# RWKV-7 time mixing on one core: a written-out order ahead of the keys, and the gate's low-rank input mixed on VectorE

## The chip, the cores and the metric

The kernel runs on one core of a Trainium2 chip. A core has a matrix engine (TensorE, PE; its weight loads are listed as PEld), a vector engine (VectorE, DVE), an activation engine (ScalarE, ACT), a general engine (GpSimd, POOL) and a queue engine (SyncE, SP) that issues the loads here. Each engine works through its own queue in order and waits on semaphores for the others. The metric is the time of one execution in microseconds (us), the median of several runs.

## The reference

A two-layer decoder trunk on 256 tokens of width 1024 in float32. Layer 0 is FFN, RWKV-7 time mixing, FFN; layer 1 is FFN, sliding-window attention, FFN. The change lies between layer 0's first FFN and the keys of its time mixing. What is computed there:

```python
h = h + 0.5 * rms_norm(swiglu(rms_norm(h, g[0]), ...), g[1])     # end of the first FFN
u = rms_norm(h, g[2])

x_prev = jnp.pad(x, ((0, 0), (1, 0), (0, 0)))[:, :-1]            # x is u
xx = x_prev - x
xr, xw, xk, xv, xa, xg = [x + xx * mu[i] for i in range(6)]
r = xr @ w_rkv[0]
k = xk @ w_rkv[1]
v = xv @ w_rkv[2]
w = -jax.nn.softplus(-(w0 + jnp.tanh(xw @ w1) @ w2)) - 0.5
decay = jnp.exp(-jnp.exp(w.astype(f32)))
a = jax.nn.sigmoid(a0 + (xa @ a1) @ a2)
g = jax.nn.sigmoid(xg @ g1) @ g2
```

w1 and a1 have 64 columns each, g1 has 128. Behind it come a scan over the tokens and the output product, which the change does not touch.

## The kernel before

The 256 tokens are worked on as two halves of 128 (index `i`), the width of 1024 as eight groups of 128 (index `k`). A product of full precision is made from three reduced ones (`mm3`: the operand is split into a high part, by a cast on ACT, and a low part, by a subtraction on DVE); the low-rank products and the values use plain float32 operands.

The stage of the change, in the order of the code:

- `ffn_tail(i)` ends the first FFN of half `i` in two PSUM banks. `post(i, ...)` squares them on ACT for the norm (L258), multiplies them by the gain on DVE (L259), takes the root through POOL (`rstd`, L239 and L242), adds to the residual `h` (L264) and squares that for the next norm (L266).
- `tm_in(i, stat)` normalises `h` (`normed`, L299), transposes it on PE (L309), writes `u` from the transposed bank with its gain, alternately on ACT (L543, even groups) and DVE (L546, odd groups), and then the difference to the token before, `xx` (L550, L552).
- `mix` makes u + xx * mu on DVE, one instruction for a group of 128 (L520): `xv` for the values, `xkm` (tag `xth`) for the keys.
- `tm_lora(i)` makes the three low-rank inputs as one matrix of 256 columns, w1, a1 and g1 side by side (`lora1`). It does not mix first: because (u + xx * mu) @ W = u @ W + xx @ (mu * W), it multiplies u by W and xx by a copy of W scaled by mu, which `tm_consts` prepared on DVE during the FFN (L511). That is 2 column groups x 8 x 2 = 32 products for a half. ACT then takes tanh into `hwa`, copies the a part into it and takes the sigmoid of the gate part into `sgT` (L583 to L585).
- `v_half(0, xv)` is the first quarter of the values: 8 products of 512 columns (L617). Its weights lie in four buffers (`wr`), which the keys' weights (`w_k`) take over one by one as these products end.
- In `tm_core`, ACT casts the keys' input to `xtl` and DVE subtracts it into `xkl` (L640, L641). PE makes the decay's pre-activation (L659, ACT's sigmoid L660), the a-gate's (L665, L667) and sums of decays (L674, exponentials L677 and L678). Then come the keys' products (L227 with `wk`), whose weights are split on ACT and DVE as they arrive (`k_split`, L314 and L315).

A scheduler with its own time estimates places the instructions of this stage on each engine. From the keys on, a written list (`STEPS`) sets the order, and `in_order` pins it: it ties each instruction of the named engines to the one before it in the program. Loads go out on SP's queue in order: a gain row for the norm after the time mixing (the buffer of the gain that L259 reads last), then the keys' weights. In the stage the first three half-chunk splits of the keys (`wk`) stand on ACT and DVE ahead of the second half's `u`.

Of the kernel before, what the change touches and what calls it, by code (L numbers as in the profile page):

```python
# [8 lines left out]
F32 = mybir.dt.float32  # L9
F32R = mybir.dt.float32r  # L10
AF = mybir.ActivationFunctionType
ALU = mybir.AluOpType
# [4 lines left out]
P = 128  # L17
D = 1024
T = 256
KT = 8  # L20
# [57 lines left out]
class Trunk:  # L78
# [426 lines left out]

    def tm_consts(self):
        nc = self.nc
        u, x = self.l1 = [self.tl("l1", [P, KT, 256], tag=f"l1{j}") for j in range(2)]
        self.load(u, self.a["lora1"].rearrange("p (k c) -> p k c", k=KT), self.mid)
        for j, c0, cw in ((1, 0, 64), (4, 64, 64), (5, 128, 128)):  # L510
            nc.vector.tensor_tensor(x[:, :, c0:c0 + cw], u[:, :, c0:c0 + cw],  # L511
                                    self.cols[:, C_MU + j * 8:C_MU + j * 8 + 8].unsqueeze(2).to_broadcast([P, KT, cw]),
                                    op=ALU.mult)
        nc.gpsimd.memset(self.hwa[64:65, 0, :], 1.0)
        nc.gpsimd.memset(self.hwa[0:64, 1, :], 0.0)
        nc.gpsimd.memset(self.hwa[0:1, 1, :], 1.0)
# [14 lines left out]

    def tm_in(self, i, stat):
        nc = self.nc
        xn, hs = stat
        r = self.rstd([hs[:, 0:1], hs[:, 1:2]], RMS_EPS)
        self.normed(i, r, None, xn)
        sl = slice(i * P, (i + 1) * P)
        for q in range(2):
# [32 lines left out]
            self.nc.tensor.matmul(b[:, j * T:(j + 1) * T], ws[k // 4][:, c0:c0 + P], xf[:, k, :], start=(k == 0),  # L571
                                  stop=(k == KT - 1))

    def tm_lora(self, i):
        nc = self.nc
        sl = slice(i * P, (i + 1) * P)
        bs = [self.bank()[:, 0:P] for _ in range(2)]
        for e, (l, x) in enumerate(zip(self.l1, (self.uT, self.xx))):
            for j in range(2):
                for k in range(KT):  # L580
                    nc.tensor.matmul(bs[j], l[:, k, j * P:(j + 1) * P], x[:, k, sl], start=(k == 0 and not e),  # L581
                                     stop=(k == KT - 1 and e == 1))
        nc.scalar.activation(self.hwa[0:64, 0, sl], bs[0][0:64, :], AF.Tanh)  # L583
        nc.scalar.copy(self.hwa[64:128, 1, sl], bs[0][64:128, :])
        nc.scalar.activation(self.sgT[:, sl], bs[1], AF.Sigmoid)  # L585

    def tm_core(self):
        nc, a, DC = self.nc, self.a, self.DC
        mm = nc.tensor.matmul
        TT, STT = nc.vector.tensor_tensor, nc.vector.scalar_tensor_tensor  # L590
# [12 lines left out]
        xv = self.tl("xt", [P, KT, P], tag="xv0")  # L603
        xkm = self.tl("xt", [P, KT, T], tag="xth")
        xkh = self.tl("xt", [P, KT, T], F32R, tag="xtl")
        self.mix(xv, 3, toks[0])
        self.mix(xkm[:, :, toks[0]], 2, toks[0])
        self.tm_lora(0)
        def v_half(n, x):
            acc = self.bank()  # L610
            ns = slice(n * 512, n * 512 + 512)

            def part(k2):
                w = self.pp.tile([P, 2, 512], F32, name=f"wr{self.uid()}", tag="wr", bufs=4)
                self.load(w, a["w_v"][2 * k2:2 * k2 + 2, :, ns].rearrange("k p c -> p k c"))
                for k in range(2):
                    mm(acc, x[:, 2 * k2 + k, :], w[:, k, :], start=(k2 + k == 0), stop=(k2 + k == 4))  # L617
            return acc, [lambda k2=k2: part(k2) for k2 in range(4)]

        def run(todo):  # L620
            for x in todo:
                x()

        acc0, todo = v_half(0, xv)
        run(todo)
        self.mix(xkm[:, :, toks[1]], 2, toks[1])
        self.tm_lora(1)
        self.close("g2k", "t4", "W1", "W2", "l1", "sh0")
        self.open("sh1")
        self.tl("sh1", [P, 24])  # L630
# [839 lines left out]
    def run(self, out):  # L1470
# [25 lines left out]
        self.load(self.cst[:, P:], a["consts"][:, P:], self.mid)  # L1496
        self.tm_consts()
        g_post = self.gain(R_NORM[(0, 1)], self.mid)
        for i in range(2):
            self.tm_in(i, self.post(i, self.ffn_tail(i), g_post, True))  # L1500
        accs, g_post = self.tm_core()

        g_pre = self.gain(R_NORM[(0, 4)])
        xt = self.new_xt("xt")
# [117 lines left out]
```

## Time and profile before

| | us |
|---|---|
| Median of 3 runs | 1054.13 |
| The three runs | 1054.13, 1053.63, 1066.59 |
| The profiled execution: its time | 1054.67 |
| The profiled execution: its span | 1052.9 |
| Mean granted TensorE clock in it | 0.993 |

The span runs from the first to the last instruction; the other 1.77 us lie around it. In a timeline row stand the start, the length, engine, line of the kernel, operation, output and input tiles, the count, and in brackets the idle time before it with the engine and line that ended it. A row of several instructions covers them all, and instructions of one engine overlap a little, so durations from start to start are the ones to add.

### The profile page before, as it was taken

To read this page: it belongs to the slowest core of one execution; us is meant where nothing else is said; L and a number is where in the kernel's file an instruction comes from. 1 tells how busy PE (TensorE), PEld (TensorE's weight loads), DVE (VectorE), ACT (ScalarE), POOL (GpSimd) and SP (SyncE) were. 2 spreads that over 40 slices of the span, in tenths; PEclk is the share of its full clock that TensorE was granted. 3 is DMA by queue.
4 is the path that set the end of the run, shared out by engine and by line. 5 is a ranking of instruction groups with operands and counts; after the bars stand their busy time and mean duration, and the time that the engine had idled before them with its cause. 6 is when DMAs were issued, how large, how long until landed. Compare 5 with 4: busy or idle time off the path is not lost.

```text
span 1052.9 us, 16152 instructions
## 1 busy us (share of the span) xinstructions
PE 1024.4 (97%) x6264; PEld 860.9 (82%) x6264; DVE 699.4 (66%) x1125; ACT 564.9 (54%) x1014; POOL 20.5 (2%) x34
## 2 busy tenths in 40 slices
PE   6999999999999999999999999999999989999997
PEld 5888888779967887888888788888877668888886
DVE  6666655527798877766665676666668866765652
ACT  6655554365245546655455665555556755655541
POOL 0000000000000001000000000000010000000000
PEclk9999999999999999999999999999999989999999
DMA  8768664034354336766663386676535127766621
GB/s 285 242 195 279 221 193 168 24 117 142 120 171 132 124 134 206 260 199 205 196 184 124 114 268 215 205 241 190 179 111 169 41 82 258 244 216 191 189 81 40
DMA packets 52668, 183.04 MB, mean 174 GB/s; under 512 B 5744, under 2 KB 6000, under 8 KB 52464
## 3 DMA queue, kind: packets, MB, share of 16 engines
q1 hardware_dynamic: 52304, 181.49, 53.3%
q8 instruction: 49, 0.80, 0.3%
q10 hardware_dynamic: 288, 0.52, 0.1%
q14 instruction: 27, 0.22, 0.1%
HBM read 180.94 MB, written 1.05 MB: 173 GB/s over the span
## 4 chain that ended last, share of the span: by engine, by line
PE 90%; ACT 3%; DVE 3%; DMA 2%; issue 1%; POOL 0%; SPq 0%; DVEq 0%; POOLq 0%; ACTq 0%
PE bk L227 35%; PE bk L362 13%; PE bt L362 13%; PE bt L363 7%; PE bk L363 7%; PE bk L571 3%; PE bk L617 2%; PE bk L581 1%; ACT W L195 1%; DMA wr<-in_w_in_dram 1%; PE bc L1002 1%; PE bk L1053 1%; PE bt L309 1%; DVE W L201 1%; DMA wr<-in_w_in_lead_dram 1%
## 5 line engine op out<-in xcount | busy, mean ns | idle before, releaser
L201 DVE TENSOR_TENSOR W<-wr,W 128x1024 fp32r<-128x1024 f32 x280 | 341.1, 1224 | 190.1 <-ACT W L195 188.7
L195 ACT CAST W<-wr 128x1024 fp32r<-128x1024 f32 x280 | 291.9, 1049 | 189.9 <-issue 94.3
L227 PE MATMUL bk<-W,g2k 128*128 128x512 f32 x1056 | 246.0, 390 | 0.0
L227 PEld LDWEIGHTS bk<-W,g2k 128*128 128x128 f32 x1056 | 195.8, 188 | 40.1
L362 PE MATMUL bk<-xtl,W 128*128 128x512 f32 x296 | 105.1, 393 | 0.0
L362 PE MATMUL bt<-xtl,W 128*128 128x512 f32 x296 | 104.4, 391 | 0.3 <-DVE xtl L350 0.3
L362 PE MATMUL bt<-xth,W 128*128 128x512 f32 x296 | 104.5, 390 | 0.0
L362 PE MATMUL bk<-xth,W 128*128 128x512 f32 x296 | 104.3, 390 | 0.0
L363 PE MATMUL bt<-xth,W 128*128 128x256 f32 x296 | 83.5, 282 | 0.0
L363 PE MATMUL bk<-xth,W 128*128 128x256 f32 x296 | 83.5, 282 | 0.0
L363 PE MATMUL bk<-xtl,W 128*128 128x256 f32 x296 | 83.4, 282 | 0.0
L363 PE MATMUL bt<-xtl,W 128*128 128x256 f32 x296 | 83.4, 282 | 0.0
L227 PE MATMUL bk<-W,xtl 128*128 128x512 f32 x216 | 61.7, 434 | 6.4 <-ACT W L195 3.3
L362 PEld LDWEIGHTS bt<-xtl,W 128*128 128x128 f32 x296 | 55.6, 188 | 12.3 <-DVE xtl L350 0.7
L362 PEld LDWEIGHTS bk<-xtl,W 128*128 128x128 f32 x296 | 55.6, 188 | 12.2
L362 PEld LDWEIGHTS bk<-xth,W 128*128 128x128 f32 x296 | 55.6, 188 | 11.6
L362 PEld LDWEIGHTS bt<-xth,W 128*128 128x128 f32 x296 | 55.5, 188 | 11.6
L227 PEld LDWEIGHTS bk<-W,xtl 128*128 128x128 f32 x216 | 42.9, 204 | 20.3 <-ACT W L195 3.8
L363 PEld LDWEIGHTS bk<-xtl,W 128*128 128x128 f32 x296 | 55.8, 189 | 1.2
L363 PEld LDWEIGHTS bt<-xth,W 128*128 128x128 f32 x296 | 55.9, 189 | 0.1
L363 PEld LDWEIGHTS bt<-xtl,W 128*128 128x128 f32 x296 | 55.9, 189 | 0.1
L363 PEld LDWEIGHTS bk<-xth,W 128*128 128x128 f32 x296 | 55.9, 189 | 0.0
(287 smaller groups left out, 1374.7 us busy)
## 6 DMA issues: line engine op xcount, KB each, us to landing
wr<-in_w_in_dram SPq DMA_DIRECT2D x148, 512.0 KB, 3.9
wr<-in_w_out_dram SPq DMA_DIRECT2D x88, 512.0 KB, 3.6
wr<-in_w_in_lead_dram SPq DMA_DIRECT2D x28, 512.0 KB, 4.1
wr<-in_w_v_dram SPq DMA_DIRECT2D x16, 512.0 KB, 3.9
gain<-in_rows_dram SPq DMA_DIRECT2D x13, 512.0 KB, 4.5
wr<-in_w_k_dram SPq DMA_DIRECT2D x8, 512.0 KB, 4.1
wr<-in_w_r_dram SPq DMA_DIRECT2D x8, 512.0 KB, 3.6
wr<-in_w_o_dram SPq DMA_DIRECT2D x8, 512.0 KB, 4.3
```

The costliest lines, as they stand in the source:

```text
L195: self.follow(nc.scalar.copy(w[:, 0, :], raw), 0)
L201: self.follow(nc.vector.tensor_tensor(w[:, 1, :], raw, w[:, 0, :], op=ALU.subtract), 1)
L227: mm = lambda *x, **y: self.nc.tensor.matmul(*x, **y, **kw)
L309: t = self.nc.tensor.transpose(b[:, k * P:(k + 1) * P], xn[:, c:c + P], self.ident)
L362: mm(banks[j], hi[:, c0:c0 + P], xt[c][:, :, k4, :], start=(k == 0), stop=False)
L363: use[0] = mm(banks[j][:, 0:T], lo[:, c0:c0 + P], xt[c][:, 0, k4, :], start=False, stop=(k == KT - 1))
L571: self.nc.tensor.matmul(b[:, j * T:(j + 1) * T], ws[k // 4][:, c0:c0 + P], xf[:, k, :], start=(k == 0), stop=(k == KT - 1))
L581: nc.tensor.matmul(bs[j], l[:, k, j * P:(j + 1) * P], x[:, k, sl], start=(k == 0 and not e), stop=(k == KT - 1 and e == 1))
L617: mm(acc, x[:, 2 * k2 + k, :], w[:, k, :], start=(k2 + k == 0), stop=(k2 + k == 4))
L1002: mm(b[r, m * N:(m + 1) * N], W[r, v - hh * 16, :], XV[r, v, :], start=True, stop=True)
L1053: mm(out[hh][half[1 - e], m * N:(m + 1) * N], lhs, UV[part][:, hh * 16 + q, :], start=(not i and part == 0 and m == 0), stop=(part == e), ...
```

## The change

The stage gets a function of its own, `front`, and its order is pinned on PE, DVE and ACT with `in_order`, from the first half's `tm_in` on. In it:

- The gate's low-rank input is mixed on DVE into a tile `xg` (8 instructions for a half), and `gate` multiplies it by g1 (8 products). `low` makes the decay and a-gate parts as before, 16 products for a half. `tm_consts` no longer scales g1, and the scaled copy is half as large.
- The second half's post-norm is written out inside `front`, cut by the mixes of the first half: four value mixes, the gain product, four value mixes, the residual, four gate mixes, the statistics, four gate mixes. `tm_in` takes the finished root.
- The value products come directly after the first half's `low`, then the first half's gate, then the second half.
- Both sigmoids of the gate come at the end, and the keys' sixteen mixes after everything else.

The diff:

```diff
 def tm_consts(self):
-        u, x = self.l1 = [self.tl("l1", [P, KT, 256], tag=f"l1{j}") for j in range(2)]
+        u, x = self.l1 = [self.tl("l1", [P, KT, 256 - 128 * j], tag=f"l1{j}") for j in range(2)]
...
-        for j, c0, cw in ((1, 0, 64), (4, 64, 64), (5, 128, 128)):
+        for j, c0, cw in ((1, 0, 64), (4, 64, 64)):
...
 def tm_in(self, i, stat):
-        xn, hs = stat
-        r = self.rstd([hs[:, 0:1], hs[:, 1:2]], RMS_EPS)
+        xn, r = stat
...
-    def tm_lora(self, i):
...
+    def front(self, acc1, g_post, xv, xkm, v00):
+        nc = self.nc
+        mm, TT, STT = nc.tensor.matmul, nc.vector.tensor_tensor, nc.vector.scalar_tensor_tensor
+        toks = [slice(0, P), slice(P, T)]
+        xg = self.tl("l1", [P, KT, P], tag="xg")
+
+        def mixes(dst, j, i, ks):
+            for k in ks:
+                self.mix_into(nc.vector, dst[:, k], j, k, toks[i])
+
+        def low(i):
+            b = self.bank()[:, 0:P]
+            for e, (l, x) in enumerate(zip(self.l1, (self.uT, self.xx))):
+                for k in range(KT):
+                    mm(b, l[:, k, 0:P], x[:, k, toks[i]], start=(k == 0 and not e), stop=(k == KT - 1 and e == 1))
+            return b
+
+        def gate():
+            b = self.bank()[:, 0:P]
+            for k in range(KT):
+                mm(b, self.l1[0][:, k, P:2 * P], xg[:, k, :], start=(k == 0), stop=(k == KT - 1))
+            return b
+
+        def low_out(i, b):
+            nc.scalar.activation(self.hwa[0:64, 0, toks[i]], b[0:64, :], AF.Tanh)
+            nc.scalar.copy(self.hwa[64:128, 1, toks[i]], b[64:128, :])
+
+        lo0 = low(0)
...
+        mixes(xv, 3, 0, range(4))
+        for n, sl in enumerate(cols):
+            nc.scalar.activation(xn[:, sl], acc1[n], AF.Square, scale=1.0 / 16, accum_out=ss[:, n:n + 1])
+            TT(og[:, sl], acc1[n], g_post[:, sl], op=ALU.mult)
+        r = self.rstd([ss[:, 0:1], ss[:, 1:2]], 4 * RMS_EPS)
+        mixes(xv, 3, 0, range(4, 8))
+        v00()
+        low_out(0, lo0)
+        for n, sl in enumerate(cols):
+            STT(h[:, sl], og[:, sl], r, h[:, sl], op0=ALU.mult, op1=ALU.add)
+            nc.scalar.activation(xn[:, sl], h[:, sl], AF.Square, scale=1.0 / 32, accum_out=hs[:, n:n + 1])
+        mixes(xg, 5, 0, range(4))
+        r = self.rstd([hs[:, 0:1], hs[:, 1:2]], RMS_EPS)
+        mixes(xg, 5, 0, range(4, 8))
+        g0 = gate()
+        self.tm_in(1, (xn, r))
+        lo1 = low(1)
+        mixes(xg, 5, 1, range(8))
+        low_out(1, lo1)
+        g1 = gate()
+        for i, b in enumerate((g0, g1)):
+            nc.scalar.activation(self.sgT[:, toks[i]], b, AF.Sigmoid)
+        for i in range(2):
+            mixes(xkm[:, :, toks[i]], 2, i, range(8))
...
 def tm_core(self, acc1, g_post, begin):
-        self.mix(xv, 3, toks[0])
-        self.mix(xkm[:, :, toks[0]], 2, toks[0])
-        self.tm_lora(0)
...
-        acc0, todo = v_half(0, xv)
-        run(todo)
-        self.mix(xkm[:, :, toks[1]], 2, toks[1])
-        self.tm_lora(1)
+        v0 = []
+
+        def v00():
+            acc, todo = v_half(0, xv)
+            v0.append(acc)
+            run(todo)
+
+        self.front(acc1, g_post, xv, xkm, v00)
+        acc0 = v0[0]
+        self.in_order(begin, "PE", "DVE", "Activation")
...
 def run(self, out):
-        for i in range(2):
-            self.tm_in(i, self.post(i, self.ffn_tail(i), g_post, True))
-        accs, g_post = self.tm_core()
+        xn, hs = self.post(0, self.ffn_tail(0), g_post, True)
+        r = self.rstd([hs[:, 0:1], hs[:, 1:2]], RMS_EPS)
+        acc1 = self.ffn_tail(1)
+        begin = len(nc.cur_bb.bb.instructions)
+        self.tm_in(0, (xn, r))
+        accs, g_post = self.tm_core(acc1, g_post, begin)
```

How it moves the engines' instructions, at three places. The rows have the line, the operation, output tile and inputs, the size and the count.

PE before, from the end of the first half's low-rank products to the start of the second's (`u`, `xx` the inputs, `l` the low-rank matrices, `bk` and `bt` PSUM banks, `xv` the values' input, `wr` their weights, `t` the normalised rows):

```order
L581 MATMUL bk_1805<-xx_100,l_252_1616 128x128 x4
L581 MATMUL bk_1806<-xx_100,l_252_1616 128x128 x6
L617 MATMUL bk_1842<-wr_1843,xv_272_1786 128x512 x2
L617 MATMUL bk_1842<-wr_1847,xv_272_1786 128x512 x2
L617 MATMUL bk_1842<-wr_1851,xv_272_1786 128x512 x2
L617 MATMUL bk_1842<-wr_1855,xv_272_1786 128x512 x2
L309 MATMUL bt_1760<-cst,t_264_1742 128x128 x4
L309 MATMUL bt_1770<-cst,t_264_1742 128x128 x4
```

PE now, from the first half's low-rank products to the first decay product (`xg` the gate's mixed input, `hwa` the low-rank output):

```order
L587 MATMUL bk_1749<-u_99,l_251_1615 128x128 x8
L587 MATMUL bk_1749<-xx_100,l_252_1616 128x128 x8
L657 MATMUL bk_1785<-wr_1786,xv_264_1745 128x512 x2
...
L593 MATMUL bk_1819<-xg_1748,l_251_1615 128x128 x8
L309 MATMUL bt_1830<-cst,t_272_1769 128x128 x4
L309 MATMUL bt_1840<-cst,t_272_1769 128x128 x4
L587 MATMUL bk_1850<-u_99,l_251_1615 128x128 x8
L587 MATMUL bk_1850<-xx_100,l_252_1616 128x128 x8
L593 MATMUL bk_1877<-xg_1748,l_251_1615 128x128 x8
L705 MATMUL bk_1955<-gain_1739,hwa 128x512
```

The low-rank products of a half went to two banks, one for decay and a-gate, one for the gate; now only the first is left beside u and xx, and the gate's eight products on `xg` follow later, the first half's between the values and the second half's transposes.

DVE before, from the first mixes to the second half's `u` (`xth` and `xkl` the keys' input and its low part, `wk` the keys' weights):

```order
L520 SCALAR_TENSOR_TENSOR xv_272_1786<-xx_100,cols,u_99 128x128 x4
L520 SCALAR_TENSOR_TENSOR xth_1787<-xx_100,cols,u_99 128x128 x3
L299 TENSOR_SCALAR t_264_1742<-h_65,rs_1755 128x512 x2
L520 SCALAR_TENSOR_TENSOR xth_1787<-xx_100,cols,u_99 128x128
L641 TENSOR_TENSOR xkl_1940<-xth_1787,xtl_1788 128x8x128
L315 TENSOR_TENSOR wk_2022<-wr_2020,wk_2022 128x512
L315 TENSOR_TENSOR wk_2038<-wr_2020,wk_2038 128x512
L315 TENSOR_TENSOR wk_2055<-wr_2053,wk_2055 128x512
L546 TENSOR_SCALAR u_99<-bt_1760,cols 128x128
```

DVE now, over the same stretch:

```order
L608 TENSOR_TENSOR t_271_1768<-bk_456,gain_1623 128x512
L239 SCALAR_TENSOR_TENSOR rs_1778<-ss_1766 128x1
L520 SCALAR_TENSOR_TENSOR xv_264_1745<-xx_100,cols,u_99 128x128 x4
L614 SCALAR_TENSOR_TENSOR h_65<-t_271_1768,rs_1778,h_65 128x512 x2
L520 SCALAR_TENSOR_TENSOR xg_1748<-xx_100,cols,u_99 128x128 x4
L239 SCALAR_TENSOR_TENSOR rs_1812<-hs_1767 128x1
L520 SCALAR_TENSOR_TENSOR xg_1748<-xx_100,cols,u_99 128x128 x4
L299 TENSOR_SCALAR t_272_1769<-h_65,rs_1812 128x512 x2
L315 TENSOR_TENSOR wk_2022<-wr_2020,wk_2022 128x512
L315 TENSOR_TENSOR wk_2038<-wr_2020,wk_2038 128x512
L315 TENSOR_TENSOR wk_2055<-wr_2053,wk_2055 128x512
L545 TENSOR_SCALAR u_99<-bt_1830,cols 128x128 x2
```

The keys' mixes and their subtraction left this stretch, the second half's post-norm and the gate's mixes came in, and the three splits of the keys' weights still stand ahead of the second half's `u`.

ACT now, from the second half's low-rank output to the decay's sigmoids (`p` their output, `xtl` the cast of the keys' input):

```order
L597 ACTIVATE hwa<-bk_1850 64x128
L598 COPY hwa<-bk_1850 64x128
L626 ACT_TABLE_LOAD
L626 ACTIVATE sgT<-bk_1819 128x128
L626 ACTIVATE sgT<-bk_1877 128x128
L686 CAST xtl_1747<-xth_1746 128x8x128
L706 ACTIVATE p_303_1954<-bk_1955 128x512
L706 ACTIVATE p_303_1954<-bk_1958 128x512
L686 CAST xtl_1747<-xth_1746 128x8x128
L706 ACTIVATE p_306_1961<-bk_1962 128x512
```

Before, the table load stood between the first half's `hwa` and `sgT`, and both casts came before the decay's sigmoids; now all three stand here, a cast ahead of each pair of sigmoids.

More of the change, by code (lines that the diff above doesn't have):

```diff
@@ L572, in feat_half @@
                                   stop=(k == KT - 1))
-    def tm_lora(self, i):
+    def front(self, acc1, g_post, xv, xkm, v00):
         nc = self.nc
[L576 to L579, printed above, removed]
-                for k in range(KT):
[L581 to L585, printed above, removed]
@@ L587, in tm_core @@
-    def tm_core(self):
+        mm, TT, STT = nc.tensor.matmul, nc.vector.tensor_tensor, nc.vector.scalar_tensor_tensor
[7 more added lines that the diff above has]
+            for e, (l, x) in enumerate(zip(self.l1, (self.uT, self.xx))):
+                for k in range(KT):
+                    mm(b, l[:, k, 0:P], x[:, k, toks[i]], start=(k == 0 and not e), stop=(k == KT - 1 and e == 1))
+            return b
@@ new lines, in gate @@
+        def gate():
[7 more added lines that the diff above has]
+        lo0 = low(0)
+        ss = self.pp.tile([P, 2], F32, name=f"ss{self.uid()}", tag="ss", bufs=6)
+        hs = self.pp.tile([P, 2], F32, name=f"hs{self.uid()}", tag="hs", bufs=4)
@@ new lines, in front @@
+        og, xn, h = self.t4(), self.t4(), self.h[1]
+        cols = [slice(0, 512), slice(512, 1024)]
+        mixes(xv, 3, 0, range(4))
[9 more added lines that the diff above has]
+            nc.scalar.activation(xn[:, sl], h[:, sl], AF.Square, scale=1.0 / 32, accum_out=hs[:, n:n + 1])
@@ new lines, in front, with tm_core @@
+        mixes(xg, 5, 0, range(4))
[11 more added lines that the diff above has]
+            mixes(xkm[:, :, toks[i]], 2, i, range(8))
+    def tm_core(self, acc1, g_post, begin):
```

## The prediction

> **What bounds the kernel now.** I read the page's busy shares first, then the chain of waits, then the engines' timelines around the changed stretch. The shares say that TensorE (PE) is the engine to watch:
>
> ```profile
> PE 1024.4 (97%) x6264; PEld 860.9 (82%) x6264; DVE 699.4 (66%) x1125; ACT 564.9 (54%) x1014; POOL 20.5 (2%) x34
> ```
>
> The chain of work that ended last shows where PE was not alone. Between the tail of the first FFN and the keys' products it runs through other engines three times (start, length, what):
>
> ```profile
> 197.26 1.38 DVE t L259 x2
> 199.37 1.41 DVE h L264 x2
> 201.10 6.07 PE bk L581 x52
> ...
> 210.64 4.12 DMA wr<-in_w_k_dram
> ```
>
> PE's timeline of that stretch (start, length, then what it did; the bracket is idle time and who ended it):
>
> ```profile
> 197.03 1.04 PE L309 MATMUL bt<-cst,t 128*128 128x128 f32 x8
> 198.23 1.95 PE L581 MATMUL bk<-u,l 128*128 128x128 f32 x12 [0.16 <-ACT u L543]
> 201.10 2.50 PE L581 MATMUL bk<-u,l 128*128 128x128 f32 x20 [0.92 <-DVE u L546]
> 203.43 3.74 PE L581 MATMUL bk<-xx,l 128*128 128x128 f32 x32
> 207.01 7.03 PE L617 MATMUL bk<-wr,xv 128*128 128x512 f32 x16
> 213.88 1.04 PE L309 MATMUL bt<-cst,t 128*128 128x128 f32 x8
> 215.72 4.11 PE L581 MATMUL bk<-u,l 128*128 128x128 f32 x32 [0.81 <-ACT u L543]
> 219.67 3.74 PE L581 MATMUL bk<-xx,l 128*128 128x128 f32 x32
> 223.24 3.60 PE L659 MATMUL bk<-gain,hwa 65*128 65x512 f32 x8
> 226.68 3.62 PE L665 MATMUL bk<-hwa,gain 128*128 128x256 f32 x16
> 230.13 3.73 PE L674 MATMUL bk<-cst,p 128*128 128x128 f32 x32
> 233.62 0.37 PE L227 MATMUL bk<-xtl,wk 128*128 128x256 f32 x1
> ```
>
> The reader is to see a stage of 36.6 us (197.03 to 233.62) in which PE is nearly full, with idle brackets of only 0.16 + 0.92 + 0.81 = 1.9 us. A product shows as two records (the 32 low-rank products of a token half are 64). What follows 233.62 begins when this stage lets it, so the question is how much earlier the keys' first product starts.
>
> **The change part by part.** *Gate on VectorE.* Each token half did 32 low-rank products, 16 on u and 16 on xx; it now does 16 for decay and a-gate and 8 for the gate, whose input is mixed beforehand. That takes 8 products from PE per half. One product costs, from the xx row, (223.24 - 219.67)/16 = 0.223 us; 16 removed are 3.6 us of PE, all on the chain. A small price goes with it: 16 mixes more on DVE. These are DVE's rows, with its key mixes (L520) and splits:
>
> ```profile
> 198.62 0.60 DVE L546 TENSOR_SCALAR u<-bt,cols 128x128 f32<-128x128 f32 x2
> 199.37 1.41 DVE L264 SCALAR_TENSOR_TENSOR h<-t,rs,h 128x512 f32<-128x512 f32 x2
> 202.63 1.13 DVE L520 SCALAR_TENSOR_TENSOR xv<-xx,cols,u 128x128 f32<-128x128 f32 x4
> 206.57 0.87 DVE L299 TENSOR_SCALAR t<-h,rs 128x512 f32<-128x512 f32 x2
> 215.43 0.69 DVE L315 TENSOR_TENSOR wk<-wr,wk 128x512 fp32r<-128x512 f32 x1 [1.03 <-ACT wk L314]
> 217.35 1.28 DVE L552 TENSOR_TENSOR xx<-u 128x512 f32<-128x512 f32 x2
> 218.55 2.18 DVE L520 SCALAR_TENSOR_TENSOR xth<-xx,cols,u 128x128 f32<-128x128 f32 x8
> 221.84 1.23 DVE L641 TENSOR_TENSOR xkl<-xth,xtl 128x1024 fp32r<-128x1024 f32 x1 [1.11 <-ACT xtl L640]
> 236.80 1.33 DVE L315 TENSOR_TENSOR wk<-wr,wk 128x512 fp32r<-128x512 f32 x2 [13.73 <-ACT wk L314]
> ...
> L511 DVE TENSOR_TENSOR l<-l,cols 128x1024 f32<-128x1024 f32 x1 | 1.2, 1215 | 0.0
> L601 DVE TENSOR_SCALAR ka<-cols 128x8 f32<-128x8 f32 x1 | 0.2, 162 | 0.0
> ```
>
> Eight mixes take 2.1 us from start to start, so 16 are 4.2 us. DVE has them to spare only because the second half's tail, from 223.07 to 236.80, is idle (the 13.73 us of the last row); the walk below shows when they bind. The removed scaling of the gate's weights (the L511 row, 1.2 us) lies far earlier beside the FFN's products, with no wait on it, and is worth nothing to the end. Two constants (the L601 row and its like) come from there into the stage, at most 0.16 us each; the low-rank products on xx cover them, and without that cover they would cost 0.3 us.
>
> *Order.* The second token half's post-norm (L607 to L615 of the change) moves behind the first half's u and xx; keys' mixes move to the end; gate mixes go where keys' mixes stood. The walk needs ACT's and the queues' rows:
>
> ```profile
> 200.22 0.63 ACT L266 ACTIVATE t<-h 128x512 f32<-128x512 f32 x1 [0.59 <-DVE h L264]
> 206.43 1.28 ACT L585 ACT_TABLE_LOAD   x1
> 207.72 0.28 ACT L585 ACTIVATE sgT<-bk 128x128 f32<-128x128 f32 x1
> 212.46 1.14 ACT L314 CAST wk<-wr 128x512 fp32r<-128x512 f32 x2 [3.52 <-DMA wr<-in_w_k_dram]
> 214.78 0.62 ACT L314 CAST wk<-wr 128x512 fp32r<-128x512 f32 x1 [1.19 <-DMA wr<-in_w_k_dram]
> 215.31 0.62 ACT L543 ACTIVATE u<-bt,cols 128x128 f32<-128x128 f32 x2
> 220.77 1.04 ACT L640 CAST xtl<-xth 128x1024 fp32r<-128x1024 f32 x1 [3.72 <-DVE xth L520]
> 224.30 0.60 ACT L660 ACTIVATE p<-bk 128x512 f32<-128x512 f32 x1 [0.58 <-PE bk L659]
> 198.78 0.55 POOL L242 TENSOR_TENSOR rs<-rs,mhalf 128x1 f32<-128x1 f32 x1 [4.54 <-DVE rs L239]
> 198.67 0.34 SPq L152 DMA_DIRECT2D gain<-in_rows_dram  x1
> 208.92 6.31 SPq L152 DMA_DIRECT2D wr<-in_w_k_dram  x5
> ```
>
> First half. PE's eight transposes stay at 197.03. ACT no longer squares the second half first, so u starts at about 197.7, but u now alternates ACT, DVE, ACT, DVE, about 0.4 us a step with the hand-over, four steps and an xx difference (0.6 us) for each group of four: the last u is ready at 200.95. Eight u products follow as they come; the eight on xx run 201.2 to 203.0. The value mixes start at 201.7 and four are done at 202.8, so the value products start at 203.0, where they began at 207.01. Their 6.87 us end at 209.9. DVE meanwhile does the second half: gain product to 204.1, four value mixes to 205.1, h to 206.5, four gate mixes to 207.5 (POOL's power, 0.55 us, and ACT's two squares of 0.63 us, from 0.85 us after h's start, lie beside them), four more to 208.6, the norm by 209.5. So the gate's eight products are ready when PE is: 209.9 to 211.7, 1.8 us.
>
> Second half. Transposes from 211.7, the first u on ACT at 212.3. ACT then copies the first value bank (128x512, 0.6 us as L660's sigmoid of that shape) between two u steps, which is exposed: DVE's last u ends at 215.6, xx at 216.2. Low-rank products end at 217.6 and the gate's, for which DVE has the last mix at 218.3, at 219.4. Against 223.24 that is 3.8 us earlier: 3.6 us of removed products and 0.2 us less waiting. The waits are thus moved, not removed: u's hand-over is late now where the FFN's post-norm and the keys' loads were.
>
> The tail. Hwa is out at 218.3, the table load runs to 219.6, and the two sigmoids end at 220.0; the third bank of the decay products waits for them and is due at 221.15, so 1.1 us are to spare. Then ACT has each half's cast of the keys ahead of two decay sigmoids, a new wait: DVE's sixteen key mixes run 218.2 to 222.4, the second cast 222.5 to 223.5, and the sigmoid behind it frees the bank that the third pair of a-gate products needs at 224.6 by 224.0. The cover is 0.6 us. DVE's splits of the keys end at about 225, before the keys' products at 229.8. From 219.4 the rows 223.24 to 233.62 follow unchanged in 10.4 us. I put the sum at -3.8 us.
>
> Three costs stand on no row. The u steps of one group alone were not recorded: at best they hide the 1.9 us of brackets altogether, at worst they cost what the first bracket of 0.92 us adds again in each half, 1.8 us; I take the steps' rows, which are the same instructions, and keep both ends. The gain load waits for DVE's gain product, so it leaves SP at 204.1 instead of 198.67 and stands directly ahead of the keys' first load, which follows the start of the value products by 1.9 us (207.01 to 208.92), now at 204.9; before, the keys' loads had the engines alone. Their second load is needed: DVE's third split and ACT's third cast stand ahead of the second half's u. It would leave 1.7 us after the first, when two more value products are done, at 206.6, land 4.12 us later at 210.75, and the split would end at 212.1, 0.65 us before the first DVE step. If the gain load holds it up by a whole load (214.78 - 212.46 = 2.3 us between two landings), 1.65 us are lost. Nearer is the row without delay, since 0.8 us pass before the keys' load and a further 1.7 us before the second; I take 0 and keep 1.65. Nothing excludes a gain there, but it can't exceed the waits already counted.
>
> The table load is the third. Its row shows 1.28 us and the sigmoid directly after it. [...]
>
> **The rivals.** *The gain load collides.* For it: same queue, 0.8 us apart. Against it: the 1.7 us between the keys' loads. The gain is 3.8 - 1.65 = 2.15 us: 1054.13 - 2.15 = 1052.0 us.
>
> *The saved products are hidden anyway.* If DVE, not PE, ends the stage, PE's saving is a wait. It speaks for it that DVE has a mix, cast and split chain at the end; against it that the split ends at 225 and the keys start at 229.8. It decides once DVE is 0.6 us late at the second cast; at 4.4 us all is gone: 1054.1 us.
>
> *Slower: ACT and DVE stand behind the keys' second load.* Both are in order, and the second half's u is queued behind cast and split. Each us by which the load lands after 211.4 costs one. From a landing of 215.2, which is 8.6 us after issue where the chain has 4.12, the change loses. The slowest loads of this size stand in the full list of DMA issues (size, median us to landing):
>
> ```profile
> gain<-in_lora_dram SPq DMA_DIRECT2D x2, 512.0 KB, 10.5
> ```
>
> At 10.5 us it lands at 217.1, 5.7 us are lost and 3.8 won: 1054.13 + 1.9 = 1056.0 us. Against it, those two were behind a queue of loads, and here only one is.
>
> *More than the products.* All brackets vanish too: 3.8 + 1.9 = 5.7 us, 1048.4 us. Against it, u's steps alternate between two engines.
>
> That the order isn't kept is none here: the rows of the built program stand as the walk has them, and outside this stage they are the same.
>
> **How the numbers follow.** The profiled execution took 1054.67 us for its span of 1052.9, so the sum gives 1050.87 in its terms. The median of the three runs, 1054.13, lies 0.54 us below, so the forecast is 1050.3 us. Chances: forecast 0.68, collision 0.15, hidden 0.07, slower 0.05, more 0.05. The range reaches from the last (1048.4, less 0.5 us between the two closest runs: 1047.9) to no gain (1054.1, up to 1054.2) and leaves out the slower case. A measurement of this kernel tells about 2%, 21 us, from no change; no case reaches that far, and 0.01 on each side is left for what I have not seen.
>
> **What would show it.** The value products start near 203, the second transposes near 211.7, the decay products near 219.4, the keys' products near 229.8; DVE's key mixes end before 222.5, and ACT's third key cast before 212. Low-rank products number 48, not 64. It is wrong if PE waits for the second half's u beyond 216, if the a-gate products wait for an ACT sigmoid behind a key cast, or if the 3.8 us seen at the keys' start are gone at the span's end.

## The result, and the profile after

| | before | after |
|---|---|---|
| Median, us | 1053.72 (20 runs) | 1048.85 (20 runs) |
| Lowest and highest run, us | 1051.70, 1066.59 | 1046.87, 1052.09 |
| Profiled execution: time, span, us | 1054.67, 1052.9 | 1048.02, 1046.2 |
| Mean granted TensorE clock in it | 0.993 | 0.997 |

The ratio of the times is 0.9941, with a 95% interval of 0.9924 to 0.9957. The change makes the kernel faster by 0.6%, 6.2 us by the ratio and 4.9 us by the medians. The forecast was 1050.3 us with 3.8 us gained. The ratio weighs the spread too: of 107 runs of the kernel before in this study 15 took over 1056 us, of 31 of the changed kernel none did.

The profile after, in the order in which the one before was read. The page's busy shares first (us, share of the span, instructions). PE has 32 records less, the 16 products; DVE has 15 instructions more:

```profile
PE 1019.8 (97%) x6232; PEld 856.4 (82%) x6232; DVE 702.6 (67%) x1140; ACT 564.3 (54%) x1014; POOL 20.5 (2%) x34
```

PE's timeline of the stage in the changed kernel (start, length, work; the bracket is idle time and who ended it):

```profile
196.81 1.03 PE L309 MATMUL bt<-cst,t 128*128 128x128 f32 x8
197.87 1.88 PE L587 MATMUL bk<-u,l 128*128 128x128 f32 x10
200.10 1.27 PE L587 MATMUL bk<-u,l 128*128 128x128 f32 x6 [0.34 <-DVE u L545]
201.21 1.95 PE L587 MATMUL bk<-xx,l 128*128 128x128 f32 x16
203.00 7.03 PE L657 MATMUL bk<-wr,xv 128*128 128x512 f32 x16
209.87 1.95 PE L593 MATMUL bk<-xg,l 128*128 128x128 f32 x16
211.65 1.04 PE L309 MATMUL bt<-cst,t 128*128 128x128 f32 x8
212.71 1.88 PE L587 MATMUL bk<-u,l 128*128 128x128 f32 x10
214.87 1.27 PE L587 MATMUL bk<-u,l 128*128 128x128 f32 x6 [0.28 <-DVE u L545]
215.98 1.95 PE L587 MATMUL bk<-xx,l 128*128 128x128 f32 x16
217.77 1.95 PE L593 MATMUL bk<-xg,l 128*128 128x128 f32 x16
219.55 3.60 PE L705 MATMUL bk<-gain,hwa 65*128 65x512 f32 x8
222.99 3.62 PE L711 MATMUL bk<-hwa,gain 128*128 128x256 f32 x16
226.44 3.73 PE L720 MATMUL bk<-cst,p 128*128 128x128 f32 x32
229.93 0.37 PE L227 MATMUL bk<-xtl,wk 128*128 128x256 f32 x1
```

The stage, from the first transposes to the keys' first product, lasts 33.12 us (196.81 to 229.93) where it lasted 36.59. That is 3.47 us of the 6.7 by which the two spans differ; the experiments look for the rest. PE's brackets name nothing but DVE's `u`, once in each half, 0.34 and 0.28 us. They show only a part of the waiting: the eight products on `u` take 3.34 us (197.87 to 201.21) and 3.27 us (212.71 to 215.98), where the eight on `xx` behind them take 1.79 from start to start. The rest lies inside the rows: the first ten records on `u` take 1.88 us in each half, as long as sixteen do on `xx`.

DVE in the same stage. Its steps on `u` shown here each wait for ACT's step before; its last key mix ends at 222.62, and the third split of the keys' weights ends 0.18 us before DVE's first step on the second half's `u`:

```profile
198.64 0.35 DVE L545 TENSOR_SCALAR u<-bt,cols 128x128 f32<-128x128 f32 x1 [0.44 <-ACT u L542]
200.48 0.35 DVE L545 TENSOR_SCALAR u<-bt,cols 128x128 f32<-128x128 f32 x1 [0.43 <-ACT u L542]
210.40 2.11 DVE L315 TENSOR_TENSOR wk<-wr,wk 128x512 fp32r<-128x512 f32 x3 [0.98 <-ACT wk L314]
212.69 0.35 DVE L545 TENSOR_SCALAR u<-bt,cols 128x128 f32<-128x128 f32 x1 [0.17 <-ACT u L542]
215.25 0.35 DVE L545 TENSOR_SCALAR u<-bt,cols 128x128 f32<-128x128 f32 x1 [0.43 <-ACT u L542]
216.24 2.18 DVE L520 SCALAR_TENSOR_TENSOR xg<-xx,cols,u 128x128 f32<-128x128 f32 x8
218.34 4.28 DVE L520 SCALAR_TENSOR_TENSOR xth<-xx,cols,u 128x128 f32<-128x128 f32 x16
222.54 2.42 DVE L687 TENSOR_TENSOR xkl<-xth,xtl 128x1024 fp32r<-128x1024 f32 x2
```

ACT and SP's queue there. ACT waits 0.28 us for the keys' second load, then for PE's transposes, so the load holds nobody up. The table load is followed by the sigmoids at once:

```profile
211.17 0.62 ACT L314 CAST wk<-wr 128x512 fp32r<-128x512 f32 x1 [0.28 <-DMA wr<-in_w_k_dram]
212.29 0.37 ACT L542 ACTIVATE u<-bt,cols 128x128 f32<-128x128 f32 x1 [0.50 <-PE bt L309]
218.53 1.28 ACT L626 ACT_TABLE_LOAD   x1
219.82 0.45 ACT L626 ACTIVATE sgT<-bk 128x128 f32<-128x128 f32 x2
223.61 1.08 ACT L706 ACTIVATE p<-bk 128x512 f32<-128x512 f32 x2
204.04 0.34 SPq L152 DMA_DIRECT2D gain<-in_rows_dram  x1
204.91 7.14 SPq L152 DMA_DIRECT2D wr<-in_w_k_dram  x5
```

### The profile page after: what moved, and what is told of

Read it like the earlier page. It is cut to its first block, busy times and chain, and to the rows that moved or that the text cites. A ratio compares the mean times of both kernels' runs of the same rounds, so it can differ in the third digit from the quotient of the medians.

```text
span 1046.2 us, 16104 instructions
## 1 busy us (share of the span) xinstructions
PE 1019.8 (97%) x6232; PEld 856.4 (82%) x6232; DVE 702.6 (67%) x1140; ACT 564.3 (54%) x1014; POOL 20.5 (2%) x34
## 4 chain that ended last, share of the span: by engine, by line
PE 90%; DVE 3%; ACT 3%; DMA 1%; issue 1%; POOL 0%; SPq 0%; DVEq 0%; POOLq 0%; ACTq 0%
PE bk L227 35%; PE bk L362 13%; PE bt L362 13%; PE bt L363 7%; PE bk L363 7%; PE bk L570 3%; PE bk L657 3%; PE bt L309 1%; ACT W L195 1%; DMA wr<-in_w_in_dram 1%; PE bc L1048 1%; PE bk L1099 1%; DVE W L201 1%; PE bk L1443 1%; PE bk L587 1%
## 5 line engine op out<-in xcount | busy, mean ns | idle before, releaser
L362 PEld LDWEIGHTS bt<-xtl,W 128*128 128x128 f32 x296 | 55.6, 188 | 12.5 <-DVE xtl L350 0.9
L227 PE MATMUL bk<-W,xtl 128*128 128x512 f32 x216 | 59.4, 421 | 6.4 <-ACT W L195 3.5
```

The lines of the kernel that those rows point to most:

```text
L227: mm = lambda *x, **y: self.nc.tensor.matmul(*x, **y, **kw)
L362: mm(banks[j], hi[:, c0:c0 + P], xt[c][:, :, k4, :], start=(k == 0), stop=False)
```

## The experiments

"Stage" is always the time from PE's first L309 transposes of the time mixing to the first product of `xtl` with `wk`, in the profiled execution. Ratios are to runs of the kernel before on the same chip.

**The kernel before, again** (c0), unaltered.

> The kernel before, unchanged, as a control. Called the stage here: from PE's first transposes of the first half (L309) to the keys' first product, 36.6 us in the first profile of before and 33.1 us after the change, a gain of 3.5 us, where the two profiles' spans differ by 6.7 us. Both theories: ratio 1.000 and stage 36.6 us. Theory C (what the change gained beyond its stage is chance: TensorE's clock at half speed in the attention's tail, and load landings): the spans of its runs scatter by some 4 us with a granted clock of 0.992 to 0.997, and this second profile need not repeat the two stretches at half clock (853 to 861 and 867 to 871 us) of the first. Theory D (the change moves the later stages, so that they run better): this profile repeats them, with 0.993.

Stage 36.72 us (197.34 to 234.06), span 1057.7, median 1054.99 us (12 runs), ratio 1.0017 [1.0001, 1.0032]. The stage repeats to 0.13 us, the span does not: 4.7 us lie elsewhere. The interval of this unaltered kernel just misses 1, so 0.2% is not told from no change here; e5 and e6 below, with ratios as near to 1, rest on their stage times. The clock at the attention's end speaks for theory C: the first profile of before was granted 0.50 from 855 to 860 us and c0 1.00 there, but 0.50 from 870 to 875 us, where the first had 0.91.

**The gate folded again, the written order kept** (e1). Both halves' gate products go back to `u` and `xx`; the gate's 16 mixes are gone:

```diff
-        for j, c0, cw in ((1, 0, 64), (4, 64, 64)):
+        for j, c0, cw in ((1, 0, 64), (4, 64, 64), (5, 128, 128)):
...
-        def gate():
+        def gate(i):
...
-            for k in range(KT):
-                mm(b, self.l1[0][:, k, P:2 * P], xg[:, k, :], start=(k == 0), stop=(k == KT - 1))
+            for e, (l, x) in enumerate(zip(self.l1, (self.uT, self.xx))):
+                for k in range(KT):
+                    mm(b, l[:, k, P:2 * P], x[:, k, toks[i]], start=(k == 0 and not e), stop=(k == KT - 1 and e == 1))
```

> The written order kept, but the gate's low-rank input folded into scaled weights again: 16 products for it in each half, no gate mixes. Theory A (PE's 16 removed products are the gain): 16 x 0.223 = 3.6 us back, stage 36.7 us, ratio to before 1.000. Rival B (the written order is the gain, DVE or the waits bind): stage 33.1 to 33.6 us, ratio 0.995.

Stage 36.69 us (196.20 to 232.89), span 1051.5, median 1053.43 us (12 runs), ratio 0.999 [0.9969, 1.0011]. PE's rows of the first gate in e1, which is 16 records longer than in the changed kernel:

```profile
209.25 1.95 PE L593 MATMUL bk<-u,l 128*128 128x128 f32 x16
211.03 1.95 PE L593 MATMUL bk<-xx,l 128*128 128x128 f32 x16
212.82 1.04 PE L309 MATMUL bt<-cst,t 128*128 128x128 f32 x8
```

The order alone is worth nothing in the stage (36.69 us against 36.59 and 36.72 of the kernel before), as theory A said. What e1 lost against the changed kernel, 3.57 us, is the price of the 16 products, 16 x 0.223 = 3.57.

**The gate's mixing alone, in the old order** (e2): the kernel before with `xg` mixed and 8 products in place of 16, placed by the scheduler.

```diff
-            for j in range(2):
-                for k in range(KT):
-                    nc.tensor.matmul(bs[j], l[:, k, j * P:(j + 1) * P], x[:, k, sl], start=(k == 0 and not e),
-                                     stop=(k == KT - 1 and e == 1))
+            for k in range(KT):
+                nc.tensor.matmul(bs[0], l[:, k, 0:P], x[:, k, sl], start=(k == 0 and not e),
+                                 stop=(k == KT - 1 and e == 1))
...
+        self.mix(self.xg, 5, sl)
+        for k in range(KT):
+            nc.tensor.matmul(bs[1], self.l1[0][:, k, P:2 * P], self.xg[:, k, :], start=(k == 0), stop=(k == KT - 1))
```

> The kernel before with the gate mixed on DVE and 8 products for it in each half, the scheduler's order kept, no other part of the change. Rival A2 (the products alone are worth it in any order): stage 33.0 us, ratio 0.995. My theory (the order makes room for the mixes): the scheduler puts the gate's mixes among the keys' mixes ahead of the values' and of the gate's products, so about 1 us is left, stage 35.6 us, ratio 0.999.

Stage 34.99 us (197.35 to 232.34), span 1049.9, median 1051.63 us (12 runs), ratio 0.9987 [0.9967, 1.0006]. PE now waits for the mixes, once in each half (PE's timeline of e2):

```profile
205.45 0.49 PE L586 MATMUL bk<-xg,l 128*128 128x128 f32 x2 [0.86 <-DVE xg L520]
220.85 1.28 PE L586 MATMUL bk<-xg,l 128*128 128x128 f32 x8 [0.81 <-DVE xg L520]
```

So 1.6 us of the 3.6 arrive without the order, more than the 1 us expected, and nothing arrives with the order alone. The written order is what lets DVE deliver: the two parts are worth more together (3.5) than apart (1.6 and 0).

**The changed code without the pinning** (e5): the line `self.in_order(begin, "PE", "DVE", "Activation")` left out.

> The changed code with the pinning of its order left out, so that the scheduler places the same instructions. PE's order stays; on DVE the second half's residual comes ahead of the first half's last u, and keys' mixes go among value and gate mixes again. If the written order is worth the 1.9 us between the gate alone (34.99) and the whole change (33.12), the stage is 34.5 to 35 us and the ratio near 0.998. If writing the code in this sequence is enough, it is 33.1 us and 0.994 to 0.996.

Stage 34.19 us (196.84 to 231.03), ratio 0.9981 [0.9964, 0.9998], median 1051.19 us (12 runs). PE's waits are like those of the kernel before, since the scheduler again puts DVE's residual of the second half (199.18) ahead of the first half's last two `u` (200.51; PE's timeline of e5):

```profile
200.91 1.38 PE L587 MATMUL bk<-u,l 128*128 128x128 f32 x10 [1.19 <-DVE u L545]
214.32 2.77 PE L587 MATMUL bk<-u,l 128*128 128x128 f32 x16 [0.72 <-ACT u L542]
```

The changed code without its pinning gave 2.4 us in the stage, 0.8 more than the mixed gate alone (e2) and a little more than expected; the pinning gave the last 1.1. PE's order did not stay as it was, against the expectation: the gate's first eight records stand in the middle of the value products (207.35, between values at 203.91 and 208.24).

**The keys' mixes early** (e4): the written order with eight of them ahead of the first half's residual and eight ahead of the second half's gate mixes.

```diff
         mixes(xv, 3, 0, range(4, 8))
         v00()
+        mixes(xkm[:, :, toks[0]], 2, 0, range(8))
...
+        mixes(xkm[:, :, toks[1]], 2, 1, range(8))
         mixes(xg, 5, 1, range(8))
...
-        for i in range(2):
-            mixes(xkm[:, :, toks[i]], 2, i, range(8))
```

> The changed kernel with the keys' sixteen mixes moved from the end of the written order to where the gate's finish: eight of them ahead of the gate's first mixes' successor work (behind the second half's norm statistics), eight ahead of the second gate's mixes. If the late place of the keys' mixes is what makes the mixed gate free, each group of eight (2.1 us on DVE) is now in front of something PE waits for: the second half's normalised rows and splits about 1.1 us late, the second gate's products about 1.1 us late, stage 35.3 us in place of 33.1, ratio about 0.9985. If DVE has slack anyway, the stage stays at 33.1 and the ratio at 0.994 to 0.996.

Stage 37.15 us (197.25 to 234.40), ratio 1.000 [0.9973, 1.0027], median 1053.14 us (12 runs). PE's three new waits in e4:

```profile
212.92 1.28 PE L593 MATMUL bk<-xg,l 128*128 128x128 f32 x8 [1.57 <-DVE xg L520]
214.71 1.09 PE L309 MATMUL bt<-cst,t 128*128 128x128 f32 x8 [0.51 <-DVE t L299]
221.86 2.33 PE L593 MATMUL bk<-xg,l 128*128 128x128 f32 x16 [0.81 <-DVE xg L520]
```

The direction was as expected, the size was not: 4.0 us were lost instead of 2.2, since the low part of the keys' input (1.23 us on DVE, from 209.96) and two splits of their weights (from 211.24) moved up with the mixes and stood ahead of the gate's last four (212.52). Where the keys' mixes stand is thus worth the whole gain of the change.

**One reader for each transposed bank** (e3): ACT writes `u` of groups 0 to 3, DVE of groups 4 to 7, where they took turns within a bank.

```diff
-                if k % 2 == 0:
+                if q == 0:
...
+        for q in range(2):
             u, xx = self.uT[:, q * 4:q * 4 + 4], self.xx[:, q * 4:q * 4 + 4]
```

The two differences `xx` follow both banks: that is a second change beside the readers.

> The changed kernel, but each transposed bank is read by one engine: ACT writes u's first four groups, DVE the last four, and the two differences xx follow. Theory (ACT and DVE take turns on one bank, 0.4 us a step, and that hand-over is what PE waits for now): the first value product starts 1.4 us earlier, the second half gains as much again, stage 30.3 us, ratio to before 0.9925. Rival (PE's products or DVE's row of mixes bind, the hand-over is hidden): stage 33.1 us, ratio 0.995.

Stage 30.49 us (196.98 to 227.47), span 1043.3, median 1046.03 us (6 runs), ratio 0.993 [0.9918, 0.9942]. It was run a second time beside the changed kernel, as e3b:

> The changed kernel with one reader for each transposed bank once more, beside the changed kernel on the same chip: stage 30.5 us, 2.6 us under the changed kernel's, ratio 0.991 to 0.994, its interval below the changed kernel's median ratio. If the 2.6 us do not reach the end, its ratio lies inside the changed kernel's interval.

Stage 30.49 us again (195.99 to 226.48), median 1045.58 us (4 runs), ratio 0.992 [0.9907, 0.9933]; the changed kernel on the same chip had 0.9948 [0.9934, 0.9962]. ACT's first four steps and PE behind them, in e3:

```profile
197.62 1.14 ACT L542 ACTIVATE u<-bt,cols 128x128 f32<-128x128 f32 x4 [4.23 <-PE bt L309]
198.04 2.15 PE L588 MATMUL bk<-u,l 128*128 128x128 f32 x16
200.03 1.95 PE L588 MATMUL bk<-xx,l 128*128 128x128 f32 x16
```

Four steps take 1.14 us on one engine, and DVE does the other bank meanwhile. In the changed kernel, taking turns, the first bank was done at 198.99 (198.64 + 0.35) and only the second at 200.83 (200.48 + 0.35), each step behind a wait of 0.4 us for the other engine, and the first bank's `xx` (0.68 us on DVE) stood between the banks. No bracket is left in PE's stage. This version beats both kernels. The rival is refuted; how the 2.6 us divide between the readers and the later `xx` is not shown, since no run moves `xx` alone.

**One reader for each bank in the kernel before** (e6). Only the condition is changed; `xx` stays where it is in the code.

> The kernel before with one edit: the first transposed bank is read by ACT alone, the second by DVE alone, where they alternated. In the kernel before, the 16 u products of a half need 3.57 us but took 5.36 in the first half (198.07 to 203.43) and 4.75 in the second (214.92 to 219.67): 3.0 us of waiting. If the hand-over between two readers of one bank is its cause, most of it goes, whatever the order: stage 34.1 to 35.1 us in place of 36.6, ratio about 0.998. If the cause there is DVE's post-norm ahead of u, the stage stays within 0.5 us of 36.6 and the ratio at 1.000.

Stage 35.24 us (196.80 to 232.04), a gain of 1.35, slightly less than the lower end of the expected 1.5 to 2.5; ratio 0.9987 [0.9975, 0.9998], median 1051.70 us (12 runs). All of it comes from the first half: its values start 8.45 us after the transposes (205.25) in place of 9.98. There the scheduler also moved DVE's residual behind its `u` (to 200.10, from 199.37 between them), so this run does not tell the hand-over from the post-norm. Besides, each engine of the kernel before does its two steps of a bank in one go (ACT 197.81 to 198.47, then DVE 198.62 to 199.22), where the changed kernel takes turns step by step. In the second half, ACT's `u` still stands behind the keys' third cast, and PE waits for it (PE's timeline of e6):

```profile
214.41 3.84 PE L581 MATMUL bk<-u,l 128*128 128x128 f32 x32 [1.26 <-ACT u L543]
```

**The changed kernel again, twice** (c1, c2), unaltered.

> The changed kernel again, unaltered. So far the stage gave 3.47 us (33.12 against 36.59) while the spans of the two profiles differ by 6.7 us and the medians by 4.9. Theory C (all behind the keys' first product is chance: when TensorE's clock is halved and when loads land): the stage is 33.1 again, the stretch from the keys' first product to the last block of products is anywhere in the 787 to 795 us that the unchanged instruction stream has shown so far, and the ratio's interval reaches 0.9967 or above (3.5 us of 1054) as often as not. Theory D (the earlier start improves later stages too): the stretch is 787 to 788 us again and the ratio is 0.994, its interval below 0.996.

> The changed kernel once more, beside the shifted one. Theory P: no stop after record 61, at most 0.2 us 32 records later; stage 33.1 to 33.4 us; ratio 0.994 to 0.996 and no run more than 4 us above the median. Theory Q says the same of this kernel.

c1: stage 33.32 us, span 1048.3, median 1049.13 us (5 runs), ratio 0.9959 [0.9947, 0.9972]. c2: stage 33.11 us, span 1049.4, median 1049.00 us (6 runs), ratio 0.9948 [0.9934, 0.9962]. To see what lies outside the stage, the chains of work that ended last were laid side by side, step by step. From the keys' first product on they agree to 0.1 us, except at three places. The table gives what each profile lost (+) or won (-) against the first profile of before at the start (when the stage begins), in the stage, and at these three:

| | start | stage | scan, 331 us | w_in load, 576 us | attention's end, 851 to 886 us | sum | span |
|---|---|---|---|---|---|---|---|
| c0 (before) | +0.3 | +0.1 | +3.8 | +1.5 | -0.9 | +4.8 | 1057.7 |
| e1 | -0.8 | +0.1 | -0.1 | -0.8 | +0.2 | -1.4 | 1051.5 |
| e6 | -0.2 | -1.4 | -0.1 | -0.5 | -1.6 | -3.8 | 1049.1 |
| after | -0.2 | -3.5 | -0.6 | -0.7 | -1.6 | -6.6 | 1046.2 |
| c1 (after) | +0.1 | -3.3 | -0.5 | +0.1 | -1.1 | -4.6 | 1048.3 |
| c2 (after) | +0.5 | -3.5 | -0.6 | -0.1 | +0.1 | -3.5 | 1049.4 |
| e3 | -0.1 | -6.1 | -0.6 | -0.1 | -2.7 | -9.6 | 1043.3 |
| e3b | -1.0 | -6.1 | -0.6 | -0.1 | -1.3 | -9.1 | 1043.7 |
| e2 | +0.3 | -1.6 | -0.4 | -0.5 | -0.9 | -3.0 | 1049.9 |
| e4 | +0.2 | +0.6 | -0.3 | -0.2 | -1.3 | -1.1 | 1051.8 |
| e5 | -0.2 | -2.4 | +9.5 | -0.8 | -2.6 | +3.5 | 1056.4 |
| f1, below | +4.3 | -3.2 | 0.0 | -0.5 | +0.2 | +0.8 | 1053.7 |

At the w_in load it is the landing that varies: 4.87 us in the first profile of before, 3.97 after, 4.92 in c1. At the attention's end it is TensorE's clock. These are stretches of 5 us (length, then busy time and instructions of PE, PEld, DVE, ACT and POOL, then the granted clock, the DMA share and GB/s), before first and after second, shifted by the 5 us that after is ahead there:

```profile
850.00:855.00 5.00, 2.56 (x13) 1.57 (x11) 2.71 (x4) 2.14 (x4) 0.00 (x0) 0.89 0.47 183
855.00:860.00 5.00, 5.00 (x12) 3.94 (x13) 3.52 (x7) 2.69 (x7) 0.81 (x2) 0.50 0.36 105
```

```profile
845.00:850.00 5.00, 2.41 (x13) 1.57 (x11) 2.75 (x4) 2.14 (x4) 0.00 (x0) 1.00 0.39 156
850.00:855.00 5.00, 5.00 (x22) 4.05 (x23) 3.49 (x7) 2.72 (x7) 0.84 (x2) 1.00 0.38 105
```

The same stop of PE was followed by 5 us at half the clock in one execution and by none in the other. c1, the same program as after, had 0.74 there. The stretch that the expectations speak of was 790.6 us in the first profile of before, 787.7 in after's, 789.2 in c1 and 790.1 in c2: theory D, which wanted 787 to 788 again, falls. What the profile of after won at the last two places is chance: executions of one and the same program differ there by as much.

The scan is another matter: the changed kernel and e3 gain 0.5 to 0.6 us there in all five profiles, e2 and e4 0.4 and 0.3, e1 and e6 next to nothing (0.1), and c0 and e5 lose much. The profiles that gain have the mixed gate in common, written order or not; e5 has it too.

**The count of PE's instructions** (f1). In the scan PE stops once, for a time in which the trace shows nothing that it waits for. The edit puts 32 records ahead of the first transposes of the whole kernel:

```diff
         b = self.tbank()
+        if not self.turned and not hasattr(self, "shifted"):
+            self.shifted = True
+            for _ in range(16):
+                self.nc.tensor.matmul(b[:, 0:8], self.ident, self.cst[:, 0:8], start=True, stop=True)
```

> The changed kernel with 16 tiny products (32 records, 8 columns each, their result overwritten) put ahead of PE's first transposes, where PE waits anyway. In the ten profiles so far PE stops once in the scan, for 0.3 to 1.2 us in which the trace shows nothing that it waits for, and always at the same count of PE's instructions from the start: after record 61 of a block of 64 products with the long program (the kernel before, e1, e6), 32 records later with the changed one, 16 products shorter (e2, e4, e5), where it is 0 to 0.7 us. Theory P (the count decides: the supply of instructions runs dry there): the stop is back after record 61 of the second block of 64, 0.35 us or more wide, and none is seen 32 records later; the keys' first product stands 33.1 to 33.4 us after the first transposes as before. Theory Q (the order or the time decides): the stop is 0 to 0.2 us, as in the changed kernel.

PE's timeline at that place, before, then f1:

```profile
329.59 1.16 PE L947 MATMUL bc<-c,GS 32*32 32x32 f32 x61
331.10 0.25 PE L947 MATMUL bc<-c,GS 32*32 32x32 f32 x3 [0.35 <-issue]
```

```profile
330.66 1.19 PE L997 MATMUL bc<-c,GS 32*32 32x32 f32 x63
332.25 0.21 PE L997 MATMUL bc<-c,GS 32*32 32x32 f32 x1 [0.40 <-issue]
```

The stop is back, 0.40 us wide, at record 63 of the same block (61 was expected), and the 0.55 us are lost again (+0.03 against the first profile of before); stage 33.35 us (201.34 to 234.69). Counted from the start of the kernel, the stop stands behind 1,997 of PE's records in before, c0, e1, e6, c1, e4 and e5, behind 1,998 in e2 and 1,999 in f1; in the other four none is seen. So the count of instructions decides where PE stops, as theory P has it, to within two records; that the supply of instructions runs dry there was the author's supposition, and no run shows it. It does not decide alone how long: with the longer program the stop cost 0.5 to 1.4 us in five profiles (before, c0, e1, e6, f1), with the shorter one 0 to 0.3 in seven and about 0.9 in e5 (from start to start, against the fastest profile at that record). The changed kernel wins about half a microsecond there because its PE program is 16 products shorter; one profile of f1 shows it. The whole kernel's time (1053.77 us in the median of 11 runs, ratio 1.0003 [0.9991, 1.0014]) says nothing on it, because the tiny products were not tiny: they took 0.22 us a record and put everything behind them 4.3 us later (PE's first rows in f1):

```profile
4.56 6.99 PE L310 MATMUL bt<-cst 128*128 128x8 f32 x32 [4.56 <-DMA cst<-in_consts_dram]
11.40 1.95 PE L313 MATMUL bt<-cst,t 128*128 128x128 f32 x8
```

## Why the prediction was right and wrong

*The products.* Right: 16 products at 0.223 us were to save 3.6 us on the chain, and e1, which puts them back, loses 3.57.

*The walk of the stage.* Right to within 0.15 us at each point it named: values at 203.00 (203.0), second transposes at 211.65 (211.7), decay products at 219.55 (219.4), keys' products at 229.93 (229.8), DVE's key mixes ended at 222.62 (before 222.5, so 0.1 late), ACT's third key cast at 211.79 (before 212). The starting point was 0.2 us earlier than taken, so the stage itself gained 3.47, not 3.8: the term "0.2 us less waiting" was mis-sized, it is -0.1. From the end of the transposes to the first `xx` product PE lost 1.8 and 1.2 us on `u` in the kernel before and 1.6 and 1.5 us in the changed one (with 1.79 us for eight products), so the hand-over cost what the old waits had cost.

*The waits are moved, not removed.* Right. e5 shows them in their old places, e2 the first of them; e3 removes them and gains 2.6 us, so the hand-over of `u`, with `xx` between the banks, was indeed what was late next. Their size was misread: the prediction took the brackets, 1.9 us, for all that could be won by them, but the rows on `u` held 3.0 us, and e3's stage lies 6.1 us below that of the kernel before, more than the 5.7 that the removed products and all brackets make.

*The costs without a row.* The gain load left at 204.04 (204.1 forecast) and the keys' loads at 204.91; the second landed near 211.1, not 210.75, and cost nobody anything. The value taken, 0, held, though the split was done 0.18 us ahead of the first DVE step rather than 0.65. The a-gate products follow the decay's without a gap, 222.99 to 226.44, so ACT's casts ahead of the sigmoids cost nothing either.

*The table load.* Right: the load takes 1.28 us, and the sigmoid starts 0.01 us after it (218.53 + 1.28 to 219.82), as the row before the change had it (206.43 + 1.28 to 207.72).

*The rivals.* The collision, the hidden products and the slower case did not come. "More than the products" gave 1048.4 us, and the median is 1048.85: the number fits, the mechanism does not. It lets all brackets vanish, and 0.34 and 0.28 us are still there; what the time has beyond the stage's 3.47 us comes from outside the stage.

*How the numbers follow.* Here the prediction failed, at one step: "A measurement of this kernel tells about 2%, 21 us, from no change". No row or run stands behind the 2%. Twenty runs of each told 0.6% from no change, with an interval of 0.17% to each side. The forecast's own 3.8 us are 0.36%, so by its own sum "faster" was what such a measurement would show, and the 0.98 that "0.01 on each side" leaves for no change belonged to a bound about ten times too wide. The three runs at hand could not have settled it, since two agreed to 0.5 us and the third lay 12.5 us above; they gave no ground for 21 us either.

*The sum to the end.* It took the rest of the kernel as unmoved. The stage's gain does pass on undiminished, but the shorter PE program wins about 0.5 us more in the scan: 3.3 to 3.5 and 0.5 to 0.6, together 3.8 to 4.1 us, repeat in all three profiles of the changed kernel. The stop stands in the profile before, 0.35 us at 331.10, outside the stage, but only the later runs tie it to the count of PE's instructions. The medians show 4.9, 4.3 and 5.2 us, 0.2 to 1.4 us more. Part of that goes with TensorE's clock: between runs of equal mean granted clock, where it is on record, the medians differ by 4.2 us at 0.995 and at 0.996 (37 runs of the kernel before against 19) and by 4.8 at 0.997 (11 against 8). What is left is not settled. Over 1056 us the changed kernel was never seen, and the two profiles that lost 4 to 9.5 us in the scan (c0, e5) are of other orders. But e5 has as many PE instructions as the changed kernel, and its stop, a bracket of 0.67 us, was merely longer. Why it varies was not found.

## What to carry to other kernels

Ask of an instruction taken from the bounding engine who must now deliver instead, and write the order so that the new supplier isn't behind work that is due later: the gate's mixes were worth 1.6 us in the scheduler's order and 3.5 in the written one, and nothing with the keys' mixes ahead of them. Where two engines empty one PSUM bank in turns and the next engine consumes in the same order, give each a bank of its own: that, with `xx` moved behind both, was worth 2.6 us here, three quarters of what the whole change brought in the stage. Don't read the brackets of a grouped row as all its waiting: set its length against that of the same number of products without waits. Before giving a chance to "no change", work out what the measurement can tell from the spread of enough runs.

## What the runs showed of the hardware

A float32 product of 8 columns cost nearly as much as one of 128: 0.22 us a record (6.99 us for 32) against 0.24 for the transposes directly behind (1.95 us for 8, the rows of f1 above). A small column count bought almost nothing there, at the start of the kernel, where both are slow: eight records of transposes took 1.04 us in the stage.

PE stops in the scan at one count of its instructions (behind 1,997 to 1,999 records), with a bracket of 0 to 1.2 us, in a stretch in which its records follow one another every 0.02 us (61 in 1.16 us). The longest stop seen (c0, PE's timeline):

```profile
332.39 0.25 PE L947 MATMUL bc<-c,GS 32*32 32x32 f32 x3 [1.19 <-issue]
```

PE's clock behind it, in stretches of 4 us of c0:

```profile
330.00:334.00 4.00, 2.81 (x114) 2.58 (x112) 1.20 (x2) 1.81 (x4) 0.00 (x0) 0.95 0.43 129
334.00:338.00 4.00, 4.00 (x69) 3.63 (x64) 0.41 (x1) 1.73 (x4) 0.00 (x0) 0.50 0.03 10
```

The same in e5, two stretches out of five that follow one another:

```profile
330.00:334.00 4.00, 4.00 (x77) 2.72 (x76) 1.27 (x2) 1.87 (x4) 0.00 (x0) 0.75 0.30 118
346.00:350.00 4.00, 4.00 (x42) 3.88 (x41) 1.63 (x2) 1.44 (x3) 0.00 (x0) 0.50 0.02 4
```

The stop itself cost at most 1.4 us, from start to start (c0); with the half clock behind it the scan lost 3.8 us in c0 and 9.5 us in e5, where the clock was 0.50 in each stretch of 4 us from 334 to 350 us though PE was busy throughout (4.00 us of 4.00). That the stop brought the half clock about is not shown: it followed the two longest stops of the thirteen profiles and none of the others, which cost up to 0.6 us. What makes PE stop at that count, no run shows. The stop at the attention's end was followed by half the clock in one execution (0.50 over the 5 us from 855 in the profile before) and by the full clock in another (1.00 over the 5 us from 850 in the profile after); what decides between them no run shows either.
